# Expert results added on chip by one-hot products, the last fourteen experts in pairs, the overflow loop at the end

## The chip, the core and the metric

One core of a Trainium2 chip runs the whole program. TensorE (PE) multiplies and transposes into eight PSUM banks, VectorE (DVE) and ScalarE (ACT) move and change what lies there, GpSimd (POOL) issues the indirect transfers, and SyncE (SP) issues the weight loads. Each engine takes its instructions in a fixed order. The metric is the device time of one execution in microseconds (us), and less is better.

## The reference

512 tokens of 1024 numbers go through a mixer, a mixture of experts, and a second block of two feed-forwards with attention between them. The change touches the mixture of experts:

```python
def run_block(args):
    xb, e = args
    return (jax.nn.silu(xb @ w_gate[e]) * (xb @ w_up[e])) @ w_down[e]
...
y = y_pad[dest] * sorted_w[:, None].astype(h.dtype)
out = jnp.zeros((n_tok, d), h.dtype).at[sorted_tok].add(y)
```

Each token goes to 2 of 32 experts (1024 assignments); an expert has gate and up weights of 1024 x 512 and down weights of 512 x 1024. All is float32.

## The kernel before

The activations stand transposed in `self.x` ([128, 8, 512]: features on partitions, eight blocks k, tokens along the row). The router counts the tokens of each expert and ranks the experts by count. `SEQ` is the order in which the experts are worked: experts 0 and 1 (fixed, so that their weights can be loaded early), then four times two small experts and a big one, then eighteen small ones.

- **Big** (ranks 0 to 5): 128 slots, products as three float32r matmuls (`mm3`, L255 to L257) on weights that ACT and DVE split into a high and a low half (`wtile`, L201 and L202).
- **Small** (ranks 6 to 31): 64 slots, plain float32 on the raw weights. The array is used as two halves of 64 columns: gate and up (`small_up`, L960), or the two output halves (`small_down`, L987), lie side by side in one bank. The profile shows each of these matmuls as two instructions.

The loop `for n, p in enumerate(SEQ)` (in `moe`) does for each expert: transpose the activation (`small_tr` L972, copied by DVE L975), start the gather of the tokens of expert n+2 (POOL L1061), transpose the tokens of expert n+1 (`small_x` L944, copied by DVE L947), do its up products, then the down products of expert n. ACT scales the result out of PSUM (L991), and POOL scatters its rows to a DRAM array `yrow` (L877), which SP had cleared during the mixer (`clear`). The results of the last three experts stay on chip. At the end `yrow` is read back, its two halves are added (L869), transposed (L1023) and added to `x`; the last three results are added by a one-hot product (`add_block`, L1013 and L1014): a matrix `sel` of 0 and 1 (`one_hot`, L1039 to L1044) carries slots back to tokens. The last result is fed into `x` block by block inside the first feed-forward (`ffn`).

The weights of an expert are six transfers of 1 MB (`mload`, L236) that SP issues in the order `wkeys`, up to 13 ahead, into the 16 buffers of `p8`; one of the 16 holds the gathered tokens. `spill` is a loop over all experts for tokens past the slots. With the reference's inputs it runs no round: the largest counts of the ranks do not pass the slots. Its entry stands after expert n = 22.

Of the kernel before, what the change touches and what calls it, by code (L numbers as in the profile page):

```python
# [9 lines left out]
I32 = mybir.dt.int32  # L10
# [22 lines left out]
NFIXED, NBIG, CAP = 2, 6, 64  # L33
ROUNDS = (T + CAP) // 128 + 1
MOE_WINDOW = 13
MOE_MORE = {0: 8, 3: 9, 5: 10, 6: 11, 7: 12}
LAST = 3
# [4 lines left out]
def sequence():  # L42

    small = list(range(NBIG, NE))
    seq = list(range(NFIXED))
    for b in range(NFIXED, NBIG):
        seq += [small.pop(0), small.pop(0), b]
    return seq + small


SEQ = sequence()
RAW = 2
# [6 lines left out]
SPILL_AT = 22  # L59
# [55 lines left out]
class Net:  # L115
    def __init__(self, tc, ctx, A, out):
# [24 lines left out]
        self.yrow = self.dr.tile([2 * T, D], F32, name="yrow")  # L141
# [188 lines left out]
    def mixer(self):  # L330
# [53 lines left out]
        for c in range(ND):  # L384
            self.clear(c)
# [167 lines left out]
    def clear(self, j):  # L553

        if j == 0:
            self.zero = self.t4([128, D])
            self.nc.gpsimd.memset(self.zero, 0.0)
        self.tc.keep_in_program_order(self.nc.sync.dma_start(self.yrow[j * 128:j * 128 + 128, :], self.zero))

# [48 lines left out]
    def moe_stream(self):  # L608
# [5 lines left out]
        for n, p in enumerate(SEQ):  # L614
            gu = [("gu"[j], p, h) for h in range(2) for j in range(2)]
            d = [("d", SEQ[n - 1], h) for h in range(2)] if n else []
            self.wkeys += d + gu if n == NFIXED else gu + d
        self.wkeys += [("d", SEQ[-1], h) for h in range(2)]
        self.windex = {k: i for i, k in enumerate(self.wkeys)}
        views, last = [], None  # L620
        for p in SEQ + [None]:
            if p is not None and p < NBIG:
# [6 lines left out]
        self.mload(MOE_MORE[0])  # L629

# [33 lines left out]
    def moe(self):  # L664
# [9 lines left out]
        hrow, yrow, table, pay, payf = self.hrow, self.yrow, self.table, self.pay, self.payf  # L674
# [82 lines left out]
        def fixed2(e):  # L757

            p = self.ps()
            for i in range(NT):  # L760
                mm(p[:, 0:3], sels[e].bitcast(F32)[:, i, :], payf[:, i, e, 0:3], start=i == 0, stop=i == NT - 1)
            nc.vector.tensor_scalar(tabs[e][:, 1:2], p[:, 0:1], float(FAR), None, op0=add)
            nc.vector.tensor_copy(tabs[e].bitcast(F32)[:, 2:4], p[:, 1:3])
# [3 lines left out]
        rank, order, big = self.ranks(cn)  # L767
# [9 lines left out]
        pf = [payf[:, :, :, c] for c in range(3)]  # L777
        nc.vector.tensor_scalar(pf[0], o2[:, :, fx], float(T), None, op0=mul)
        nc.vector.tensor_tensor(pf[0], pf[0], self.payi.bitcast(F32)[:, :, 0:1].to_broadcast([128, NT, NFIXED]), op=add)
        nc.vector.tensor_tensor(pf[2], o2[:, :, fx], bc(d, NFIXED), op=mul)  # L780
        nc.vector.tensor_tensor(pf[1], o1[:, :, fx], bc(ds, NFIXED), op=mul)
        nc.vector.tensor_tensor(pf[1], pf[1], pf[2], op=add)
        nc.vector.tensor_copy(pf[2], rt.rearrange("p (i o) -> p i o", o=1).to_broadcast([128, NT, NFIXED]))
# [7 lines left out]
        nc.vector.scalar_tensor_tensor(rowr, rk3, CAP - 0.5, all4(big), op0=ALU.is_ge, op1=mul)  # L791
        nc.vector.tensor_tensor(rowr, rowr, all4(rank), op=add)
        nc.vector.scalar_tensor_tensor(row, rk3, float(NE), rowr, op0=mul, op1=add)
# [23 lines left out]
        nc.vector.tensor_scalar(ce, cn[:, 0:NE], CAP + 0.5, None, op0=ALU.is_gt)  # L817
        nc.vector.scalar_tensor_tensor(ce, big, 1.0 / NE, ce, op0=mul, op1=mul)
# [11 lines left out]
        tab2 = self.keep("tab2", [128, NE, 4], I32)  # L830
        for h in range(2):
            nc.gpsimd.dma_start(tab2[64 * h:64 * h + 64].rearrange("p e c -> p (e c)"), trow[0:64, :])
        nc.gpsimd.dma_start(self.ordd, order[0:1, :])
        for p in range(NFIXED, NE):
            tabs[p] = tabb[:, p, :] if p < NBIG else tab2[:, p, :]

        def gather(n):
            p = SEQ[n]
# [5 lines left out]
        def up(n):  # L844
            p, xt = SEQ[n], self.xts[n % 2]
            if p < NBIG:
                return self.expert_up(self.split_next, self.expert_x(xt), tabs[p])
            return self.small_up(p, self.small_x(xt), tabs[p])
        a = up(0)
        last, ys = [], []  # L850
        for n, p in enumerate(SEQ):
            tab = tabs[p]
# [5 lines left out]
            if n == NE - LAST:  # L858
                for i in range(NT):
                    ya = self.t8([128, 2, D])  # L860
                    nc.gpsimd.dma_start(ya, yrow.rearrange("(j i p) d -> i p j d", j=2, p=128)[i])
                    ys.append(ya)
            if n == NE - 2:
# [3 lines left out]
            if n == NE - 1:  # L867
                for ya in ys:
                    tc.keep_in_program_order(nc.vector.tensor_tensor(ya[:, 0], ya[:, 0], ya[:, 1], op=add))  # L869
                self.add_rows(ys)  # L870
                self.add_small(last)
            if p < NBIG:
                y, tb = self.expert_down(self.split_next, aT, tab), tab
            else:
                y, tb = self.small_down(p, aT, tab), tab[0:CAP]
            if n < NE - LAST:
                nc.gpsimd.indirect_dma_start(yrow, bass.IndirectOffsetOnAxis(ap=tb[:, 1:2], axis=0), y, None,  # L877
                                             bounds_check=2 * T - 1, oob_is_err=False)
            else:
                last.append(self.small_rows(y, tab))  # L880
            if n == SPILL_AT:
                self.spill(rounds, trow)
            self.presplit(self.wnext + SPLITS)
        self.last = last[LAST - 1:]

    def spill(self, rounds, trow):
# [3 lines left out]
        with tc.For_i(1, nr, 1) as b:  # L890
            with tc.For_i(0, NE, 1) as p:
                A, B, C = (self.t8([128, 2048], dt) for dt in (F32R, F32, F32))
                P, Q = self.t2(), self.t2()
                G, Y = self.t4([128, 1024], F32R), self.t4([128, 1024])
                U, V = ([self.wp.tile([128, 2, 512], F32R, name=nm, tag=nm) for nm in ("wh", "wl")] for _ in range(2))
                X, Z = self.ps(), self.ps()
                self.own = {"t8": [A, B, C, B, C, B, C, A], "t4": [G, Y], "t2": [P, Q, G[:, 0:512]],
# [11 lines left out]
                self.add_experts([self.expert_rows(self.expert_down(st.__next__, aT, tb), tb)])  # L909
                self.own = None  # L910

    def ranks(self, cn):
# [21 lines left out]
        rank, big = self.keep("rank", [128, NE]), self.keep("big", [128, NE])  # L934
        nc.vector.tensor_copy(rank, p[:, NE:2 * NE])
        nc.vector.tensor_scalar(big, rank, NBIG - 0.5, float((128 - CAP) * NE), op0=ALU.is_ge, op1=mul)
        return rank, self.order, big
# [12 lines left out]
    def small_up(self, e, xT, tab):  # L950
# [27 lines left out]
    def small_down(self, e, aT, tab):  # L978
        nc = self.nc
        tf = tab.bitcast(F32)  # L980
        p = self.ps()
        for h in range(2):
            w = self.raw_next(("d", e, h))
            for q in range(2):
                k = 2 * h + q
                for j in range(2):
                    nc.tensor.matmul(p[CAP * j:CAP * j + CAP, :], aT[:, k * CAP:k * CAP + CAP],  # L987
                                     w[:, q, j * 512:j * 512 + 512], start=k == 0, stop=k == 3)
        y = self.t4([128, D])
# [4 lines left out]
    def small_rows(self, y, tab):  # L994

        nc = self.nc
        sel = self.one_hot(tab)
        both = self.t8([128, 2, D], F32R)
        yT, hi = both[:, 0], both[:, 1]
        nc.scalar.copy(hi[0:CAP], y)  # L1000
        nc.vector.tensor_tensor(yT[CAP:128], y, hi[0:CAP].bitcast(F32), op=ALU.subtract)
        nc.scalar.copy(yT[0:CAP], y)
        return yT, sel
# [11 lines left out]

    def add_rows(self, ys):

        nc = self.nc
        for i, ya in enumerate(ys):
            for h in range(2):  # L1020
                p = self.ps()
                for k in range(4):
                    nc.tensor.transpose(p[:, k * 128:k * 128 + 128],  # L1023
                                        ya[:, 0, (4 * h + k) * 128:(4 * h + k) * 128 + 128], self.ident)
# [698 lines left out]
```

## Time and profile before

| | us |
|---|---|
| median of 3 runs (2073.02 to 2077.95) | 2075.43 |
| the profiled execution, its own time | 2075.37 |
| its span, first to last instruction | 2073.6 |
| PE busy | 1917.7 (92%) |
| DVE busy | 1145.2 (55%) |
| ACT busy | 736.0 (35%) |
| mixture of experts, about | 455 to 1010 |

Busy shares are averages over stages. In the stage of the experts the profile gives 410 GB/s of transfers, elsewhere mostly 20 to 110. The profiled execution is within 0.1 us of the median.

### The profile page before, as it was taken

How to read it: one execution, taken by the hardware profiler on the slowest of the kernel's cores; microseconds unless marked ns; L12 is line 12 of the kernel's file. 1: busy time of each engine (PE TensorE's matmuls, PEld its weight loads, DVE VectorE, ACT ScalarE, POOL GpSimd, SP SyncE). 2: the span in 40 equal slices, each digit the busy share in tenths (PEclk: the TensorE clock that was granted, in tenths of full speed). 3: DMA queues.
4: the chain of work that ended last, by engine and by line, in shares of the span. 5: the costliest groups of instructions: out<-in, count | busy, mean ns of one | idle time of the engine just before them, and what ended most of it. 6: DMA issues, size and time to landing. Idle time of an engine off the chain costs nothing.

```text
span 2073.6 us, 24135 instructions
## 1 busy us (share of the span) xinstructions
PE 1917.7 (92%) x9267; PEld 1429.9 (69%) x9267; DVE 1145.2 (55%) x1905; ACT 736.0 (35%) x1143; POOL 86.4 (4%) x106
## 2 busy tenths in 40 slices
PE   7999999979988998496799999999989999999997
PEld 5898888866444432132688888888777778888886
DVE  7999987456444311011864443248999855444323
ACT  5334335336333311011432322235448543232221
POOL 0000001002111111010000000000000000000000
PEclk9999999979999999698899999999999999999998
DMA  9121233539999999798222224230111112222311
GB/s 332 52 102 41 102 122 111 228 112 343 406 409 413 406 408 412 315 418 368 82 83 100 92 92 156 97 133 19 49 31 62 47 69 90 101 92 92 147 56 41
DMA packets 65463, 354.15 MB, mean 171 GB/s; under 512 B 10523, under 2 KB 11451, under 8 KB 32832
## 3 DMA queue, kind: packets, MB, share of 16 engines
q1 hardware_dynamic: 56304, 334.06, 41.6%
q0 software_dynamic: 7744, 14.71, 2.1%
q10 hardware_dynamic: 1296, 3.79, 0.5%
q8 instruction: 74, 1.21, 0.2%
q14 instruction: 45, 0.37, 0.1%
HBM read 345.41 MB, written 17.91 MB: 175 GB/s over the span
## 4 chain that ended last, share of the span: by engine, by line
PE 48%; DVE 3%; DMA 3%; ACT 2%; issue 1%; DVEq 0%; ACTq 0%; SPq 0%
PE ps L255 14%; PE ps L257 14%; PE ps L256 14%; DMA t<-in_w_up 2%; PE ps L960 2%; PE ps L1564 1%; DMA t<-in_w_down 1%; PE ps L987 1%; ACT t L1538 1%; PE ps L1551 1%; DVE wl L202 0%; DVE t L202 0%; ACT wh L201 0%; ACT t L201 0%; PE ps L1569 0%
## 5 line engine op out<-in xcount | busy, mean ns | idle before, releaser
L255 PE MATMUL ps<-t,wl 128*128 128x512 f32 x1728 | 685.3, 397 | 16.8 <-ACT t L206 16.4
L256 PE MATMUL ps<-t,wh 128*128 128x512 f32 x1728 | 681.4, 394 | 1.0 <-DVE t L207 1.0
L257 PE MATMUL ps<-t,wh 128*128 128x512 f32 x1728 | 681.6, 394 | 0.0
L201 ACT CAST wh<-t 128x1024 fp32r<-128x1024 f32 (+3 forms) x321 | 325.4, 1016 | 697.1 <-PE ps L257 511.8
L202 DVE TENSOR_TENSOR wl<-t,wh 128x1024 fp32r<-128x1024 f32 (+3 forms) x321 | 379.0, 1182 | 237.3 <-ACT wh L201 233.3
L255 PEld LDWEIGHTS ps<-t,wl 128*128 128x128 f32 x1728 | 325.8, 189 | 94.8 <-ACT t L206 16.8
L256 PEld LDWEIGHTS ps<-t,wh 128*128 128x128 f32 x1728 | 326.0, 189 | 76.1 <-DVE t L207 1.5
L257 PEld LDWEIGHTS ps<-t,wh 128*128 128x128 f32 x1728 | 325.6, 188 | 75.8
L960 PE MATMUL ps<-t,t 128*64 128x512 f32 x832 | 202.0, 617 | 35.3 <-DVE t L947 15.8
L960 PEld LDWEIGHTS ps<-t,t 128*64 128x64 f32 x832 | 64.3, 141 | 156.6 <-issue 106.0
L402 DVE SCALAR_TENSOR_TENSOR t<-t,vec,t 128x512 f32<-128x512 f32 x240 | 165.4, 743 | 0.4
L255 PE MATMUL ps<-wh,t 128*128 128x256 f32 (+2 forms) x440 | 144.6, 329 | 8.3 <-DVE t L202 8.3
L965 DVE SCALAR_TENSOR_TENSOR t<-ps,tab,t 64x512 f32<-64x512 f32 x26 | 19.6, 756 | 233.8 <-ACT t L963 233.8
L256 PE MATMUL ps<-wl,t 128*128 128x256 f32 (+2 forms) x440 | 142.8, 325 | 0.0
L257 PE MATMUL ps<-wh,t 128*128 128x256 f32 (+2 forms) x440 | 141.9, 322 | 0.0
L963 ACT ACTIVATE t<-ps,tab 64x512 f32<-64x512 f32 x26 | 17.7, 681 | 239.8 <-PE ps L960 239.8
L987 PE MATMUL ps<-t,t 128*64 128x512 f32 x416 | 100.1, 596 | 2.2 <-DMA t<-in_w_down 2.2
L255 PEld LDWEIGHTS ps<-wh,t 128*128 128x128 f32 x440 | 83.7, 190 | 21.2 <-DVE t L202 9.9
L1195 DVE TENSOR_TENSOR t<-ps,rbc 128x512 f32<-128x512 f32 x44 | 30.3, 689 | 115.2 <-PE ps L257 115.2
L257 PEld LDWEIGHTS ps<-wh,t 128*128 128x128 f32 x440 | 83.7, 190 | 7.0
L256 PEld LDWEIGHTS ps<-wl,t 128*128 128x128 f32 x440 | 83.8, 190 | 6.4 <-DVE wl L202 0.2
L201 ACT CAST t<-t 128x512 fp32r<-128x512 f32 (+2 forms) x102 | 62.7, 620 | 56.9 <-DVE t L1196 26.6
(323 smaller groups left out, 1557.5 us busy)
## 6 DMA issues: line engine op xcount, KB each, us to landing
t<-in_w_down SPq DMA_DIRECT2D x80, 1024.0 KB, 16.1
t<-in_w_gate SPq DMA_DIRECT2D x64, 1024.0 KB, 19.7
t<-in_w_up SPq DMA_DIRECT2D x64, 1024.0 KB, 17.8
t<-in_w_in SPq DMA_DIRECT2D x24, 1024.0 KB, 6.0
t<-in_w_gate SPq DMA_DIRECT2D x44, 512.0 KB, 3.5
t<-in_w_up SPq DMA_DIRECT2D x44, 512.0 KB, 3.5
t<-in_w_down SPq DMA_DIRECT2D x8, 768.0 KB, 4.5
t<-in_w_qi SPq DMA_DIRECT2D x4, 1040.0 KB, 4.7
```

What stands on the lines that cost most here:

```text
L201: nc.scalar.copy(hi, src)
L202: nc.vector.tensor_tensor(lo, src, hi.bitcast(F32), op=ALU.subtract)
L255: mm(acc, a[1], b[0], start=first, stop=False)
L256: mm(acc, a[0], b[1], start=False, stop=False)
L257: mm(acc, a[0], b[0], start=False, stop=last)
L402: nc.vector.scalar_tensor_tensor(y[c], src, w, y[c], op0=mul, op1=add)
L960: nc.tensor.matmul(p[CAP * j:CAP * j + CAP, :], xT[:, k * CAP:k * CAP + CAP], ws[j][:, q, :], start=k == 0, stop=k == ND - 1)
L987: nc.tensor.matmul(p[CAP * j:CAP * j + CAP, :], aT[:, k * CAP:k * CAP + CAP], w[:, q, j * 512:j * 512 + 512], start=k == 0, stop=k == 3)
L1195: nc.vector.tensor_tensor(a, accs[1], rbc, op=mul)
L1538: nc.scalar.activation(part(i), part(i), AF.Exp, bias=nm[:, i:i + 1], scale=scale, accum_out=su[:, i:i + 1])
L1551: nc.tensor.transpose(tb[b][:, o + (i - s) * 128:o + (i - s) * 128 + 128], P[:, self.PO[i] + s * 128:self.PO[i] + s * 128 + 128], self.ident)
L1564: self.nc.tensor.matmul(acc[64 * h:64 * h + 64, s * 128:512], V[h](s), PT[h][:, self.SO[s]:self.SO[s] + 512 - s * 128], start=s == 0, stop ...
```

## The change

1. **Results stay on chip.** `yrow`, its clearing, the scatter and the read back are gone. A small result is split into a high half (ACT) and a low half (DVE) that fill 128 partitions, a big one into two tiles. In the next iteration DVE makes its one-hot matrix, and the up products of the expert after next carry, after each block k, the add of block k: a 128x512 matmul (two for a big result) and a DVE add into `x`.
2. **Pairs.** Ranks 18 to 31 run as seven pairs, 32 slots for each expert, four array parts of 32 columns side by side. So there are 25 units in place of 32.
3. **The overflow loop** stands between the up and the down products of the last unit, after the last weights and two feed-forward weights were asked for.

```diff
+    small = [(p,) for p in range(NBIG, NSMALL)]
+    seq = [(p,) for p in range(NFIXED)]
     for b in range(NFIXED, NBIG):
-        seq += [small.pop(0), small.pop(0), b]
-    return seq + small
+        seq += [small.pop(0), small.pop(0), (b,)]
+    return seq + small + [(p, p + 1) for p in range(NSMALL, NE, 2)]
...
-            self.clear(c)
...
+            ys = []
+            if y is not None:
+                sel = self.one_hot(tabs[SEQ[n - 1][0]])
+                ys = [(t, sel) for t in y]
             aT = self.expert_tr(a) if p < NBIG else self.small_tr(a)
-            if n + AHEAD < NE:
+            if n + AHEAD < NU:
                 gather(n + AHEAD)
-            if n + 1 < NE:
-                a = up(n + 1)
...
+            if n + 1 < NU:
+                a = up(n + 1, ys)
+            else:
                 self.fst = self.ffn_stream(A["w1_gate"], A["w1_up"], A["w1_down"])
                 self.fst.load(FFN_FIRST)
-                self.fst.split(2)
...
+                self.add_small(ys)
+                self.fst.split(1)
+                for key in self.down_keys(unit):
+                    self.raw_next(key)
                 self.spill(rounds, trow)
+            y = self.expert_down(self.split_next, aT, tab) if p < NBIG else self.small_down(unit, aT, tab)
...
+        c = CAP // len(unit)
         for h in range(2):
-            ws = [self.raw_next((nm, e, h)) for nm in "gu"]
+            ws = [(CAP * j + c * i, c * i, self.raw_next(("gu"[j], e, h))) for i, e in enumerate(unit) for j in range(2)]
             for q in range(4):
                 k = 4 * h + q
-                for j in range(2):
-                    nc.tensor.matmul(p[CAP * j:CAP * j + CAP, :], xT[:, k * CAP:k * CAP + CAP], ws[j][:, q, :],
+                for o, i, w in ws:
+                    nc.tensor.matmul(p[o:o + c, :], xT[:, k * CAP + i:k * CAP + i + c], w[:, q, :],
                                      start=k == 0, stop=k == ND - 1)
+                also(k)
...
+        y = self.t4([128, D], F32R)
         for j in range(2):
-            nc.scalar.mul(y[0:CAP, j * 512:j * 512 + 512], p[CAP * j:CAP * j + CAP], tf[CAP * j:CAP * j + CAP, 2:3])
-        return y[0:CAP]
...
+            nc.scalar.mul(y[s, c], p[s], w2[s])
+            nc.vector.scalar_tensor_tensor(y[o, c], p[s], w2[s], y[s, c].bitcast(F32), op0=ALU.mult,
+                                           op1=ALU.subtract)
+        return [y]
```

**On DVE**, from one small expert to the next. Before, between the gating product (L965) and the copy of the next tokens (L947) there is one copy of the activation (L975):

```order
L965 SCALAR_TENSOR_TENSOR t_5682<-ps,tab_3628,t_5680 64x512
L975 COPY t_5708<-ps 128x256
L947 COPY t_5722<-ps 128x512
L965 SCALAR_TENSOR_TENSOR t_5760<-ps,tab_3628,t_5758 64x512
L975 COPY t_5786<-ps 128x256
L947 COPY t_5800<-ps 128x512
```

Now the low half of the result (L999) and the one-hot matrix (L1018 to L1023) stand ahead of both copies (the tokens' copy is L944 here), and the eight adds (L1012) behind them:

```order
L965 SCALAR_TENSOR_TENSOR t_5944<-ps,tab_3617,t_5942 64x512
L999 SCALAR_TENSOR_TENSOR t_5959<-ps,tab_3617,t_5959 64x512 x2
L1018 TENSOR_SCALAR tokf<-tab_3617 128x1
L1020 TENSOR_SCALAR toff<-cc,tokf 128x4
L1023 TENSOR_SCALAR t_5968<-cc,toff 128x128 x4
L975 COPY t_5978<-ps 128x256
L944 COPY t_5992<-ps 128x512
L1012 TENSOR_TENSOR x<-x,ps 128x512 x8
L965 SCALAR_TENSOR_TENSOR t_6063<-ps,tab_3617,t_6061 64x512
```

The copy that the next up products read has moved behind eight instructions that belong to the result before.

**On PE**, the up products of one small expert. Before, the two halves follow one another, all with 64 columns:

```order
L972 MATMUL ps<-cc,t_5760 128x64 x4
L944 MATMUL ps<-cc,t_3001 128x64 x8
L987 MATMUL ps<-t_5613,t_5708 64x512 x4
L960 MATMUL ps<-t_5656,t_5800 64x512
L960 MATMUL ps<-t_5658,t_5800 64x512
L960 MATMUL ps<-t_5656,t_5800 64x512
L960 MATMUL ps<-t_5658,t_5800 64x512
```

Now a 128-column add (L1011) stands after each two (L959 are the up, L992 the down products):

```order
L992 MATMUL ps<-t_5826,t_5978 64x512 x4
L972 MATMUL ps<-cc,t_6063 128x64 x4
L941 MATMUL ps<-cc,t_2990 128x64 x8
L959 MATMUL ps<-t_5886,t_6111 64x512
L959 MATMUL ps<-t_5888,t_6111 64x512
L1011 MATMUL ps<-t_6087,t_6078 128x512
L959 MATMUL ps<-t_5886,t_6111 64x512
L959 MATMUL ps<-t_5888,t_6111 64x512
L1011 MATMUL ps<-t_6087,t_6078 128x512
```

So PE goes from 64-column parts to the whole array and back eight times in an expert.

**On PE at the end of the experts.** Before, the read-back rows are transposed (L1023) and two results added (L1013) ahead of the last down products. Now the add of the unit before (L1011) and the entry of the overflow loop (L882, L883) stand there:

```order
L1011 MATMUL ps<-t_7224,t_7215 128x512 x8
L882 TENSOR_LOAD rounds
L883 COMPARE_AND_BRANCH
L883 UNCONDITIONAL_BRANCH x2
...
L992 MATMUL ps<-t_7130,t_7234 32x512 x2
L992 MATMUL ps<-t_7132,t_7234 32x512 x2
```

The 32 transposes are gone, and the loop's entry came from n = 22 to here.

## Rows read from the trace of the kernel before

**Rows 1.** Windows: busy of PE, PEld, DVE, ACT, POOL, then PE clock, transfer share, GB/s.

```profile
566.00:613.00 47.00, 41.88 (x204) 22.98 (x204) 19.94 (x21) 19.23 (x24) 6.50 (x8) 0.99 1.01 410
760.00:838.00 78.00, 64.47 (x288) 21.75 (x286) 8.24 (x13) 10.80 (x17) 8.37 (x9) 1.00 1.02 412
850.00:870.00 20.00, 3.14 (x16) 1.88 (x18) 1.12 (x2) 0.00 (x0) 0.96 (x1) 0.50 0.42 163
```

**Rows 2.** Waits of PE from 519 to 711 us: total, times, longest.

```profile
PE ps L960 <- DVE t L947: 12.6, 8, 3.8
PE ps L255 <- DVE t L202: 5.6, 4, 1.4
```

**Rows 3.** Timeline, one small expert to the next: start, length, engine, what, idle before.

```profile
927.19 3.63 PE L987 MATMUL ps<-t,t 128*64 128x512 f32 x16
...
928.14 0.76 DVE L965 SCALAR_TENSOR_TENSOR t<-ps,tab,t 64x512 f32<-64x512 f32 x1 [7.95 <-ACT t L963]
...
930.86 1.38 ACT L991 ACTIVATE t<-ps,tab 64x512 f32<-64x512 f32 x2 [2.75 <-PE ps L987]
...
931.24 0.42 DVE L975 COPY t<-ps 128x256 f32<-128x256 f32 x1 [2.34 <-PE ps L972]
...
931.75 0.69 DVE L947 COPY t<-ps 128x512 f32<-128x512 f32 x1
...
932.54 7.09 PE L960 MATMUL ps<-t,t 128*64 128x512 f32 x32 [0.83 <-ACT t L991]
...
939.43 1.92 PE L987 MATMUL ps<-t,t 128*64 128x512 f32 x8
```

**Rows 4.** Timeline of PE, up products of small experts, 519 to 749 us.

```profile
519.30 7.09 PE L960 MATMUL ps<-t,t 128*64 128x512 f32 x32 [1.16 <-DVE t L947]
...
566.05 7.09 PE L960 MATMUL ps<-t,t 128*64 128x512 f32 x32 [1.16 <-DVE t L947]
...
613.91 9.31 PE L960 MATMUL ps<-t,t 128*64 128x512 f32 x32 [3.79 <-DVE t L947]
...
646.46 7.09 PE L960 MATMUL ps<-t,t 128*64 128x512 f32 x32 [0.78 <-DVE t L947]
...
663.58 10.07 PE L960 MATMUL ps<-t,t 128*64 128x512 f32 x32 [3.37 <-DVE t L947]
...
748.15 7.09 PE L960 MATMUL ps<-t,t 128*64 128x512 f32 x32 [0.83 <-ACT t L991]
```

**Rows 5.** Timeline of DVE: first and last instructions of one one-hot matrix.

```profile
952.54 0.15 DVE L1039 TENSOR_SCALAR tokf<-tab 128x1 f32<-128x1 int32 x1
...
953.00 0.88 DVE L1044 TENSOR_SCALAR t<-cc,toff 128x128 fp32r<-128x128 f32 x4
```

**Rows 6.** Timeline of PE where 64-column products give way to 128-column ones.

```profile
510.44 1.03 PE L960 MATMUL ps<-t,t 128*64 128x512 f32 x4
...
511.39 0.50 PE L255 MATMUL ps<-wh,t 128*128 128x512 f32 x1
...
511.73 0.39 PE L256 MATMUL ps<-wl,t 128*128 128x512 f32 x1
```

**Rows 7.** Timeline of PE at the overflow loop.

```profile
866.08 0.69 PE L972 MATMUL ps<-cc,t 64*128 64x64 f32 x4 [28.96 <-SPq L890]
```

**Rows 8.** Timeline of PE, end of the experts and start of the feed-forward.

```profile
968.98 1.94 PE L987 MATMUL ps<-t,t 128*64 128x512 f32 x8 [1.49 <-DMA t<-in_w_down]
...
995.15 3.97 PE L1013 MATMUL ps<-t,t 128*128 128x512 f32 x16
...
999.05 3.65 PE L987 MATMUL ps<-t,t 128*64 128x512 f32 x16
...
1006.61 0.47 PE L1013 MATMUL ps<-t,t 128*128 128x512 f32 x1 [3.90 <-DVE t L1001]
...
1015.44 0.39 PE L255 MATMUL ps<-t,wl 128*128 128x512 f32 x1
```

**Rows 9.** Timeline of POOL, first gather after the tables.

```profile
484.98 0.99 POOL L1061 DMA_INDIRECT t<-hrow,tab  x1 [4.51 <-PE ps L1071]
```

More of the change, by code (lines that the diff above doesn't have):

```diff
@@ L42, in sequence @@
 def sequence():
[L44 to L45 removed]
+    small = [(p,) for p in range(NBIG, NSMALL)]
+    seq = [(p,) for p in range(NFIXED)]
     for b in range(NFIXED, NBIG):
[L47 to L48 removed]
+        seq += [small.pop(0), small.pop(0), (b,)]
+    return seq + small + [(p, p + 1) for p in range(NSMALL, NE, 2)]
 SEQ = sequence()
+NU = len(SEQ)
 RAW = 2
@@ L629, in moe_stream, with down_keys @@
         self.mload(MOE_MORE[0])
+    def down_keys(self, unit):
+        return [("d", p, h) for h in range(2) for p in unit]
     def mload(self, n):
@@ L673, in moe @@
         rt = self.rstd([self.hsq], D, "rtok")
-        hrow, yrow, table, pay, payf = self.hrow, self.yrow, self.table, self.pay, self.payf
+        hrow, table, pay, payf = self.hrow, self.table, self.pay, self.payf
         for i in range(NT):
@@ L766, in moe @@
             self.gather(self.xts[e], tabs[e])
-        rank, order, big = self.ranks(cn)
+        rank, order, less = self.ranks(cn)
         gs = small("gs", 1)
@@ L776, in moe @@
         nc.vector.tensor_tensor(d, ds, d, op=mul)
[L777 to L783, printed above, removed]
+        pf = [payf[:, :, :, c] for c in range(2)]
+        nc.vector.tensor_tensor(pf[1], o2[:, :, fx], bc(d, NFIXED), op=mul)
+        nc.vector.tensor_tensor(pf[0], o1[:, :, fx], bc(ds, NFIXED), op=mul)
+        nc.vector.tensor_tensor(pf[0], pf[0], pf[1], op=add)
+        nc.vector.tensor_copy(pf[1], rt.rearrange("p (i o) -> p i o", o=1).to_broadcast([128, NT, NFIXED]))
         for e in range(NFIXED):
@@ L790, in all4 @@
             return t.rearrange("p (o e) -> p o e", o=1).to_broadcast([128, NT, NE])
-        nc.vector.scalar_tensor_tensor(rowr, rk3, CAP - 0.5, all4(big), op0=ALU.is_ge, op1=mul)
-        nc.vector.tensor_tensor(rowr, rowr, all4(rank), op=add)
-        nc.vector.scalar_tensor_tensor(row, rk3, float(NE), rowr, op0=mul, op1=add)
+        nc.vector.tensor_tensor(rowr, rk3, all4(less), op=add)
+        nc.vector.scalar_tensor_tensor(rowr, rowr, 127.5, all4(less), op0=ALU.is_ge, op1=mul)
+        nc.vector.tensor_tensor(rowr, rowr, rk3, op=add)
+        nc.vector.scalar_tensor_tensor(row, rowr, float(NE), all4(rank), op0=mul, op1=add)
         payfl = pay.bitcast(F32)
@@ L816, in moe @@
         ce = self.keep("ce", [128, NE])
-        nc.vector.tensor_scalar(ce, cn[:, 0:NE], CAP + 0.5, None, op0=ALU.is_gt)
-        nc.vector.scalar_tensor_tensor(ce, big, 1.0 / NE, ce, op0=mul, op1=mul)
+        nc.vector.tensor_tensor(ce, cn[:, 0:NE], less, op=add)
+        nc.vector.scalar_tensor_tensor(ce, ce, 128.5, less, op0=ALU.is_gt, op1=mul)
         nc.vector.tensor_tensor(ce, cn[:, 0:NE], ce, op=add)
@@ L842, in gather, with up, also @@
                 self.gather(self.xts[n % 2][0:CAP], tabs[p][0:CAP])
[L844 to L848, printed above, removed]
-        a = up(0)
-        last, ys = [], []
-        for n, p in enumerate(SEQ):
-            tab = tabs[p]
+        def up(n, ys=()):
+            unit, xt = SEQ[n], self.xts[n % 2]
+            tab = tabs[unit[0]]
+            def also(k):
+                if ys:
+                    self.add_block(ys, k)
+            if unit[0] < NBIG:
+                return self.expert_up(self.split_next, self.expert_x(xt), tab, also)
+            return self.small_up(unit, self.small_x(xt), tab, also)
@@ L867, in moe @@
[L867 to L880, printed above, removed]
@@ L933, in ranks @@
         nc.vector.tensor_copy(self.order, p[:, 0:NE])
-        rank, big = self.keep("rank", [128, NE]), self.keep("big", [128, NE])
+        rank, less, t = (self.keep(nm, [128, NE]) for nm in ("rank", "less", "lesst"))
         nc.vector.tensor_copy(rank, p[:, NE:2 * NE])
-        nc.vector.tensor_scalar(big, rank, NBIG - 0.5, float((128 - CAP) * NE), op0=ALU.is_ge, op1=mul)
-        return rank, self.order, big
+        nc.vector.tensor_scalar(less, rank, NBIG - 0.5, 64.0, op0=ALU.is_ge, op1=mul)
+        nc.vector.tensor_scalar(t, rank, NSMALL - 0.5, 32.0, op0=ALU.is_ge, op1=mul)
+        nc.vector.tensor_tensor(less, less, t, op=add)
+        return rank, self.order, less
     def small_x(self, xt):
@@ L948, in small_x, with small_up @@
         return xT
-    def small_up(self, e, xT, tab):
+    def small_up(self, unit, xT, tab, also):
         nc = self.nc
@@ L1046, in one_hot @@
         return sel
-    def add_experts(self, ys):
-        nc = self.nc
-        n = 2 * len(ys)
-        for k in range(ND):
-            p = self.ps()
-            for j in range(n):
-                yT, sel = ys[j // 2]
-                nc.tensor.matmul(p, yT[:, 1 - j % 2, k * 128:k * 128 + 128], sel, start=j == 0, stop=j == n - 1)
-            nc.vector.tensor_tensor(self.x[:, k, :], self.x[:, k, :], p, op=ALU.add)
     def gather(self, xt, tab):
```

119 lines of the change are left out of this document (50 added, 69 removed).

## The prediction

> **What bounds the kernel now.** I read the windows by stage first. In the stage of the experts the transfers are busy all the time (share 1.01 to 1.02 at 410 to 412 GB/s), and PE is busy for 41.88 of 47 us and 64.47 of 78 us [rows 1]. Both are near full, so I asked what PE waits for. In the first part, with the big experts, the list of waits names no transfer, only DVE: 12.6 us for the copy of the tokens, 5.6 us for the split tokens of a big expert [rows 2]. So there the chain of PE and DVE sets the pace, with the transfers just keeping up.
>
> How long that chain is shows in the timeline. From one small expert's down products to the next's, with the weights there, it is 939.43 - 927.19 = 12.24 us [rows 3]: down 3.63, then 1.72 us until the next up starts, in which DVE copies the activation and the tokens, then 6.9 us of up. The weights of an expert are 6 x 1.05 MB, at 412 GB/s 15.3 us (2.55 us for each). So PE and DVE have 3 us to spare for each small expert. A group of two small and one big takes 566.05 - 519.30 = 46.75 us in its clean form [rows 4], against 3 x 15.3 = 45.9 us of weights: nothing to spare. This is the place to cost the change: what it adds to the chain of a unit, and what the weights' buffers can hide.
>
> **Parts that cost nothing, and their cover.** The clearing of `yrow` lies in the mixer, where the engines don't read it; without it nothing waits less. POOL issues four more table loads before the first gather; I take 0.99 us for each, that of a gather, and the 4.51 us that POOL idles there [rows 9] cover them; without cover they would cost 4 us once. SP reads all ranks' expert numbers early; it does so up to 13 transfers ahead. The fixed experts' tables lose an instruction or two.
>
> **What each up product gains, on PE.** A result's add is eight 128x512 matmuls: sixteen took 3.97 us [rows 8], so 0.25 each, 2.0 us for a small result and 4.0 for a big one.
>
> PE also changes between 64-column parts and the whole array, eight times there and back. One way: the last pairs start 0.43 us apart, from 510.44 and 510.87 the next slot is 511.30; the 128-column product starts at 511.39 and its follower 0.34 later in place of 0.23 [rows 6], so 0.20. The other way: sixteen adds from 995.15 would leave the next slot at 998.97, and the 64-column product starts at 999.05 [rows 8]; with the slower second pair I take 0.13. Together 0.33, times 8 = 2.6 us for a small expert; for a big one nothing, its products have 128 columns. Below lies 0, if this is paid only where other waits hide it; above, double, if the early loading of weights is lost too. [...]
>
> **What the hand-over gains, on DVE.** The order shows that the tokens' copy now waits behind the low half of the result and its one-hot matrix, and these wait for the down products. Worked from the end of down at 930.82 with rows 3: ACT's first half 0.04 + 0.69 (1.38 for two), two DVE halves of 0.76 (the length of L965, which has that form), the one-hot matrix 953.88 - 952.54 = 1.34 [rows 5], copies 0.42 + 0.69, 0.1 to PE: 935.6, where up started at 932.54. That is 3.1 us more, with PE idle. Next to a big expert a split of weights may stand in between too; I leave it out. Into a big expert the order puts the tokens' split ahead of the one-hot matrix; there I add nothing.
>
> **What the longer idle costs in clock.** After short hand-overs (0.78 and 1.16 us idle) up takes 7.09 us. [...]
>
> **Sum until the first pair.** A small up with a small result added: 2.0 + 2.6 + 3.1 + 2.6 = 10.3 us; with a big result 12.3; a big up 2.0. From unit 2 to the first pair (unit 18) there are 6, 6 and 4 of these, and the hand-over into the pair: 61.8 + 73.8 + 8 + 3.1 = 147 us. The two long waits of before with their slow ups go away (about 5 us saved net). So the first pair's up starts 142 us after 748.15 [rows 4], at 890.
>
> A small expert then takes 22.5 us and a group 71 us, far above the 15.3 and 45.9 of their weights. The transfers run ahead until all 15 free buffers hold weights, then idle.
>
> **The pairs.** At 890, of the 86 transfers still to be used (7 x 12 and the 2 down weights of unit 17) 15 have landed; 71 x 2.55 = 181 us bring the last at 1071. PE keeps up if four 32-column parts run together as two do now: 22.5 us for a pair against 12 x 2.55 = 30.6. If they ran two by two, up and down would take 6.9 + 3.6 more: 33.0, and I add 7 x 2.4 = 17 us; I take the first. The removed scatter (at most 4.2 MB, 10 us) and the stall of the transfers at the overflow loop (20 us x 0.58 = 11.6 us lost [rows 1]) would have helped only where transfers are the bound: the 181 us have neither in them.
>
> **The end.** Before, from the last weights at 968.98 it is 46.5 us to a full stream of the feed-forward at 1015.44 [rows 8]: waiting for the read-back, transposes, adds. After: the two feed-forward weights 2.5 us (1 MB), the loop's entry 3 us (an estimate; transfers had drained a little before PE came back at 866.08 [rows 7]), down products 6 us at the low clock, result and one-hot 3.7, and the 8.8 us from 1006.61 to 1015.44 as now: 24 us. That is 22 us saved. The stream starts at 1071 + 24 = 1095, 79.5 us later than before; from there on nothing changes. On the profiled 2075.4, which is the median, this gives **2155 us**.
>
> In short, the end and the loop give back some 62 us in all (1015.44 - 748.15 - 181 - 24), and what the units before the pairs lose beyond that is the loss: lag - 62.
>
> **The rivals.**
>
> *The modes change freely and the clock holds* (chance 0.12). For it: one up after 1.16 us idle kept its clock, and TensorE can load weights ahead. Against it: rows 4 and 6. Then 12 x (2.6 + 2.6) = 62 us fall away: 2093.
>
> *The transfers stay the bound* (0.14), the other side. This needs the new hand-over to lie under other work, so that each of the 16 units before the pairs gains less than 62 / 16 = 3.9 us; from there it decides. For it: the transfers are full now, and a small expert has 3 us to spare. Against it: adds of 2 to 4 us and a hand-over of 3.1 are in the order of the instructions, already 5 and more. The last weight would land at 968.98 - 11.6 - 10 = 947, the stream start at 971: 44 us faster, 2031.
>
> *Pairs run two by two* (0.10): 2172. [...] No row here has four parts.
>
> *The change also runs the overflow loop* (0.02): an expert of rank 18 or later with over 32 tokens would bring a round over 32 experts, 32 x 15.3 = 490 us: about 2640. The reference's own inputs give these ranks at most 20 tokens.
>
> **How the numbers follow.** My forecast, a slower kernel at 2155, has 0.59; 0.03 go to no change, between the rivals (lag near 62). Its own range comes from the clock (0 to 3.0), the modes (0 to double) and the buffers (three more or fewer, 8 us): 2110 to 2200 when not all err one way. The full range reaches down past the free-mode rival to 2085 and up to 2200; below it lie the transfer-bound case and no change, above it the loop, 0.19 in all. Faster by over 0.2% (about what a measurement of this kernel can tell) 0.14, within it 0.03, slower 0.83.
>
> **What the profile after would show.** Right: from 530 to 890 us a transfer share near 0.65, PE waiting for the copy of the tokens some 3 to 4 us in each unit, small experts 20 to 23 us apart, a clock below 1 in these windows; in the pairs a share of 1.0 and PE waiting for weights; no wait at the old place of the loop, and about 24 us from the last weight to the full stream. Wrong: small experts 15 to 16 us apart and a transfer share of 1.0 from 530 on (then the hand-over is hidden), or ups of about 9 us with adds in them (then modes and clock are free), or pairs over 31 us apart with the weights there.

## The result, and the profile after

The changed kernel takes 2153.52 us (median of 4 runs, 2150.93 to 2158.33), the kernel before 2076.65 us beside it: ratio 1.0376, 95% interval 1.0352 to 1.0399. It is 3.8% slower, and 1.5 us from the 2155 predicted. The profiled execution has a span of 2151.2 us.

The windows by stage, of the same stretches as [rows 1] and then of the two parts of the stage (columns as there):

```profile
566.00:613.00 47.00, 38.23 (x147) 15.90 (x146) 29.26 (x47) 11.29 (x14) 1.93 (x2) 0.85 0.74 282
760.00:838.00 78.00, 65.62 (x256) 29.43 (x254) 45.48 (x79) 17.73 (x22) 3.72 (x4) 0.87 0.71 270
850.00:870.00 20.00, 15.46 (x48) 4.12 (x50) 9.70 (x19) 1.36 (x2) 0.93 (x1) 0.83 0.68 256
530.00:890.00 360.00, 304.64 (x1218) 131.03 (x1218) 210.82 (x351) 83.61 (x103) 15.10 (x16) 0.89 0.72 276
890.00:1059.00 169.00, 119.10 (x722) 34.69 (x722) 60.01 (x117) 12.95 (x19) 3.72 (x4) 0.89 1.01 419
```

Where the transfers were full before, their share is now 0.72 until the pairs begin; from then on it is 1.01. DVE is busy for 29.26 of 47 us where it was for 19.94. The clock is below 1 in all of them. In the third stretch the stall of the overflow loop is gone.

PE's waits from 519 to 711 us, as in [rows 2] (total, times, longest):

```profile
PE ps L959 <- DVE t L944: 22.3, 5, 4.7
PE ps L255 <- DVE t L202: 2.9, 3, 1.0
```

Five waits for the tokens' copy take 22.3 us, 4.5 each, where eight took 12.6. One hand-over between two single experts shows why, in the timeline, as in [rows 3]. In the changed kernel L992 are the down products, L998 and L999 the result's halves on ACT and DVE, L1018 to L1023 the one-hot matrix, L975 and L944 the copies of activation and tokens, L959 the up, L1011 and L1012 the adds on PE and DVE:

```profile
825.77 0.60 PE L992 MATMUL ps<-t,t 128*64 128x512 f32 x2
...
826.42 0.69 ACT L998 ACTIVATE t<-ps,tab 64x512 fp32r<-64x512 f32 x1 [3.54 <-PE ps L992]
...
827.14 0.74 DVE L999 SCALAR_TENSOR_TENSOR t<-ps,tab,t 64x512 fp32r<-64x512 f32 x1 [2.84 <-ACT t L998]
...
827.91 0.68 ACT L998 ACTIVATE t<-ps,tab 64x512 fp32r<-64x512 f32 x1 [0.81 <-DVE t L999]
828.63 0.76 DVE L999 SCALAR_TENSOR_TENSOR t<-ps,tab,t 64x512 fp32r<-64x512 f32 x1 [0.75 <-ACT t L998]
...
829.86 0.87 DVE L1023 TENSOR_SCALAR t<-cc,toff 128x128 fp32r<-128x128 f32 x4
830.76 0.42 DVE L975 COPY t<-ps 128x256 f32<-128x256 f32 x1
831.10 0.68 DVE L944 COPY t<-ps 128x512 f32<-128x512 f32 x1
...
831.84 1.98 PE L959 MATMUL ps<-t,t 128*64 128x512 f32 x4 [4.58 <-DVE t L944]
...
834.47 1.98 PE L959 MATMUL ps<-t,t 128*64 128x512 f32 x4
...
836.81 1.08 PE L959 MATMUL ps<-t,t 128*64 128x512 f32 x4
...
838.25 1.08 PE L959 MATMUL ps<-t,t 128*64 128x512 f32 x4
...
845.42 1.94 PE L992 MATMUL ps<-t,t 128*64 128x512 f32 x8
```

Down ends at 826.37, the next up starts at 831.84: 5.47 us, where it was 1.72. ACT's second half (827.91) waits for DVE's first, and the tokens' copy stands last. The up then has two steps of some 2.5 us (834.47 - 831.84 = 2.63, 836.81 - 834.47 = 2.34; granted clock 0.50 and 0.60) and six of 1.44 (838.25 - 836.81; clock 1.00), 0.58 above the 0.86 of a step without an add (6.89 / 8 in [rows 3]).

The end, as in [rows 8]:

```profile
1058.84 1.91 PE L992 MATMUL ps<-t,t 128*32 128x512 f32 x12 [1.42 <-DMA t<-in_w_down]
...
1065.31 3.54 PE L1011 MATMUL ps<-t,t 128*128 128x512 f32 x8 [4.56 <-DVE t L1023]
...
1066.11 4.87 DVE L1012 TENSOR_TENSOR x<-x,ps 128x512 f32<-128x512 f32 x8 [0.49 <-PE ps L1011]
...
1072.79 6.55 PE L992 MATMUL ps<-t,t 128*32 128x512 f32 x32 [3.95 <-DVEq L883]
...
1083.87 0.77 PE L1011 MATMUL ps<-t,t 128*128 128x512 f32 x1 [4.53 <-DVE t L1023]
...
1092.68 0.40 PE L256 MATMUL ps<-t,wh 128*128 128x512 f32 x1
```

The full stream of the feed-forward starts at 1092.7 where it started at 1015.44: 77.2 us later. That is the whole difference, 2151.2 - 2073.6 = 77.6 us of span.

### The profile page after: what moved, and what is told of

Read it like the earlier page. It is cut to its first block, busy times and chain, and to the rows that moved or that the text cites. A ratio compares the mean times of both kernels' runs of the same rounds, so it can differ in the third digit from the quotient of the medians.

```text
span 2151.2 us, 24425 instructions
## 1 busy us (share of the span) xinstructions
PE 1967.4 (91%) x9375; PEld 1420.6 (66%) x9375; DVE 1300.3 (60%) x2234; ACT 716.3 (33%) x1116; POOL 48.7 (2%) x69
## 5 line engine op out<-in xcount | busy, mean ns | idle before, releaser
L202 DVE TENSOR_TENSOR wl<-t,wh 128x1024 fp32r<-128x1024 f32 (+3 forms) x321 | 378.1, 1182 | 203.7 <-ACT wh L201 201.0
L257 PEld LDWEIGHTS ps<-t,wh 128*128 128x128 f32 x1728 | 325.4, 188 | 76.1
L959 PE MATMUL ps<-t,t 128*32 128x512 f32 (+1 forms) x832 | 201.8, 696 | 93.5 <-DVE t L944 87.6
L1012 DVE TENSOR_TENSOR x<-x,ps 128x512 f32<-128x512 f32 x200 | 133.0, 685 | 163.4 <-PE ps L1011 163.4
L1011 PEld LDWEIGHTS ps<-t,t 128*128 128x128 f32 x248 | 48.2, 215 | 145.5 <-issue 129.7
L959 PEld LDWEIGHTS ps<-t,t 128*32 128x32 f32 (+1 forms) x832 | 35.6, 133 | 159.8 <-DVE t L944 93.3
L963 ACT ACTIVATE t<-ps,tab 64x512 f32<-64x512 f32 x19 | 12.9, 681 | 338.1 <-PE ps L959 338.1
L1011 PE MATMUL ps<-t,t 128*128 128x512 f32 x248 | 108.5, 505 | 9.1 <-DVE t L1023 9.1
L992 PE MATMUL ps<-t,t 128*32 128x512 f32 (+1 forms) x416 | 80.0, 629 | 8.6 <-DMA t<-in_w_down 4.7
```

Of the source, the lines that this page charges most:

```text
L202: nc.vector.tensor_tensor(lo, src, hi.bitcast(F32), op=ALU.subtract)
L257: mm(acc, a[0], b[0], start=False, stop=last)
L959: nc.tensor.matmul(p[o:o + c, :], xT[:, k * CAP + i:k * CAP + i + c], w[:, q, :], start=k == 0, stop=k == ND - 1)
L992: nc.tensor.matmul(p[o:o + c, :], aT[:, k * CAP + i:k * CAP + i + c], w[:, q, j * 512:j * 512 + 512], start=k == 0, stop=k == 3)
L1011: self.nc.tensor.matmul(p, yT[:, k * 128:k * 128 + 128], sel, start=j == 0, stop=j == n - 1)
L1012: self.nc.vector.tensor_tensor(self.x[:, k, :], self.x[:, k, :], p, op=ALU.add)
```

## The experiments

**The theory.** Each unit before the pairs costs PE and DVE more than its weights take to come: adds, eight changes of mode (from 64-column parts to the whole array and back), a hand-over with DVE in it, and the clock that falls in the wait. What is lost until the first pair comes back only in part. **Rivals:** modes and clock are free; the transfers, the pairs or the loop did it. Each run is timed against the kernel before on the same chip (medians 2076.24, 2075.99 and 2077.24 in the three series of four kernels, in the order below).

| run | us (median) | ratio to before, 95% interval |
|---|---|---|
| the change | 2153.52 | 1.0376 [1.0352, 1.0399] |
| noadd | 2047.75 | 0.9862 [0.9845, 0.9878] |
| parts16 | 2118.15 | 1.0211 [1.0193, 1.0229] |
| late | 2127.02 | 1.0244 [1.0227, 1.0261] |
| warm | 2166.28 | 1.0430 [1.0412, 1.0447] |
| warm5 | 2129.36 | 1.0260 [1.0243, 1.0277] |
| mixed | 2155.19 | 1.0381 [1.0363, 1.0398] |
| first_late | 2084.93 | 1.0042 [1.0030, 1.0055] |
| first_late_mixed | 2048.36 | 0.9865 [0.9849, 0.9882] |
| mixed3 | 2117.44 | 1.0199 [1.0182, 1.0216] |
| best3 | 2073.74 | 0.9987 [0.9977, 0.9997] |
| best3_mixed | 2051.34 | 0.9887 [0.9870, 0.9903] |
| loop_in | 2157.11 | 1.0392 [1.0374, 1.0409] |

**noadd: the price of adding at all.**

```diff
+                if n + 1 == NU:
                     sel = self.one_hot(tabs[SEQ[n - 1][0]])
                     ys = [(t, sel) for t in y]
```

> Leaves out the adds to x of all units but the next to last and the last, with their one-hot matrices; the two halves of each result are still made. Theory (chain of the units before the pairs): each small up loses 2.0 us of adds, 2.6 us of mode changes and 1.34 us of one-hot matrix, 5.9 of 10.3 us; the lag at the first pair falls from 130 to about 50 us, a single expert takes 16 to 17 us in place of 22.7, and the time is about 2063 (down to 2031 if the shorter idle also keeps the clock; then the transfers are full from 530 on). Rival (the pairs, the moved loop or the halves on DVE made it slower): within 15 us of 2153.

2048, some 15 us under the 2063 expected and faster than before. A window of it:

```profile
530.00:830.00 300.00, 253.62 (x1254) 119.62 (x1251) 114.20 (x135) 87.14 (x109) 16.02 (x17) 0.94 0.97 386
```

And PE's waits from 500 to 860 us (L960 is the up here; the lines of the experiments are shifted by a few):

```profile
PE ps L960 <- DVE t L945: 21.7, 11, 2.5
PE ps L960 <- DMA t<-in_w_up: 11.4, 10, 2.3
```

The share is back at 0.97, and PE waits for weights as well as for DVE. So the pairs, the moved loop and the halves are not what made the kernel slower; the adds and what comes with them are. With weights there, a single expert takes 12.9 us.

**parts16 and late: the modes, taken away in two ways.** In the first the adds run in the parts of the ups:

```diff
-            self.nc.tensor.matmul(p, yT[:, k * 128:k * 128 + 128], sel, ...)
+            for o in range(0, 128, c):
+                self.nc.tensor.matmul(p[o:o + c, :], yT[:, k * 128 + o:k * 128 + o + c], sel, ...)
```

> The adds inside small ups run as products of the width of the ups themselves (two 64-column or four 32-column parts), so PE changes no mode there; results and one-hot matrices are bfloat16 for it (the halves keep about 16 bits of the result). Same number of adds, same order. Theory: a step of a small up goes from 1.43 to 1.10 us, 2.6 us less for each of the 12 small ups before the pairs, 31 us in all: about 2122. Rival (the modes change freely and the 0.57 us of an add in a step is the add itself): step 1.43, time 2153.

In the second they stand behind the up, after `a` is made:

```diff
                     nc.tensor.matmul(p[o:o + c, :], ...)
-                also(k)
...
         nc.vector.scalar_tensor_tensor(a[0:CAP], ...)
+        for k in range(ND):
+            also(k)
```

> The eight adds stand in one row behind a small up in place of one behind each step. Theory: one change of mode there and back in place of eight, 7 x 0.33 = 2.3 us less for each of the 12 small ups before the pairs; the hand-over stays: about 2126. Rival (modes are free): 2153; it may be slower if the down products now wait for the eight adds' banks on DVE (8 x 0.67 us).

Both came out as the theory has it: 35 and 27 us less. PE in parts16, three steps with an add each:

```profile
809.42 1.02 PE L960 MATMUL ps<-t,t 128*64 128x512 f32 x4
810.28 0.38 PE L1013 MATMUL ps<-t,t 128*64 128x512 bf16 x2
810.49 1.03 PE L960 MATMUL ps<-t,t 128*64 128x512 f32 x4
811.35 0.38 PE L1013 MATMUL ps<-t,t 128*64 128x512 bf16 x2
811.57 1.02 PE L960 MATMUL ps<-t,t 128*64 128x512 f32 x4
```

A step is 1.07 us in place of 1.44 with the add still in it. Parts16 also changes the type of the adds, so by itself it might show a type; late keeps the type and the number and gains nearly as much. But with the changes of width late also saves changes of type. Parts16 still goes from f32 to bf16 and back at each step without the price; whether float32r has a share in it, or the loading of a 128-column weight, no run separates. The up of late and its adds:

```profile
811.53 9.68 PE L959 MATMUL ps<-t,t 128*64 128x512 f32 x32 [4.64 <-DVE t L944]
821.14 2.11 PE L1012 MATMUL ps<-t,t 128*128 128x512 f32 x8
```

Eight adds take 2.07 us (823.21, the next down, less 821.14), 0.26 each. The up without them takes 9.68 us after 4.64 us of waiting, and 7.09 in [rows 4] after short waits. I put these 2.6 us down to the clock, which in the changed kernel stood at 0.50 and 0.60 in the two steps after such a wait (above).

**warm and warm5: the clock, with the wait left in.** Extra products on constants fill the wait, ten in warm and five in warm5:

```diff
+        if len(unit) == 1:
+            p = self.ps()
+            for i in range(10):
+                nc.tensor.matmul(p[0:CAP, 0:456], self.cc[:, 0:CAP], self.cc[:, 0:456], start=True, stop=True)
```

> Ten extra 64-column products on constants (3.8 us at full clock) stand between the tokens' transposes and a single small expert's up, where PE waits 4.6 us for DVE. Theory: they run in the wait, the clock stays 1, and an up loses its slow first steps: 2.1 to 2.6 us less for each of the 12 small ups before the pairs, 25 to 31 us: about 2125, granted clock near 1 from 530 to 860. Rival (the slow first steps come from something other than the idle, or clock costs nothing): 2153 or, as the extra products get in the way, more.

2166, slower than the changed kernel. Ten filled 7.5 us, more than the wait: each is two passes on PE, and I had counted one. (In the row below five products stand as ten.) The slow steps were gone (from 799.23 to 807.84 us the steps of an up take 1.43 to 1.45 us, and the granted clock is 1.00 from 550 to 850 us), but the overhang cost more.

> As the run with ten extra products, with five: one of them took 0.76 us there and not 0.38, so that ten filled 7.5 us, 2.9 us more than the wait of 4.6. Five take 3.8 us and end within the wait. Theory: the clock stays 1 and each of the 12 small ups before the pairs loses its slow first steps, 1.5 to 2.4 us, 18 to 29 us in all: 2124 to 2135. Rival (the clock level costs nothing on the path, since the first steps are slow for another reason): 2153.

2129, in the range. PE in warm5:

```profile
807.13 4.04 PE L955 MATMUL ps<-cc 128*64 128x456 f32 x10
811.78 1.08 PE L963 MATMUL ps<-t,t 128*64 128x512 f32 x4 [0.61 <-DVE t L944]
812.78 0.49 PE L1015 MATMUL ps<-t,t 128*128 128x512 f32 x1
813.21 1.08 PE L963 MATMUL ps<-t,t 128*64 128x512 f32 x4
```

The first step takes 1.43 us (813.21 - 811.78) like the others, the mean clock from 530 to 860 us is 0.99 where the changed kernel has 0.89, and 24 us are gained, though the up still starts 5.5 us after the down (811.78, and 802.66 + 3.65). The clock is a cost of its own. The two windows, the changed kernel first:

```profile
530.00:860.00 330.00, 279.27 (x1100) 124.40 (x1102) 197.43 (x328) 81.57 (x100) 14.17 (x15) 0.89 0.73 278
530.00:860.00 330.00, 316.86 (x1298) 138.88 (x1296) 207.20 (x346) 82.81 (x102) 14.20 (x15) 0.99 0.78 298
```

**first_late: the hand-over.** On top of late, the result's halves and the one-hot matrix (a function `evict`, called later) come after the tokens' copy:

```diff
-                sel = self.one_hot(tabs[SEQ[n - 1][0]])
-                ys = [(t, sel) for t in y]
...
+            xT = self.expert_x(xt) if unit[0] < NBIG else self.small_x(xt)
+            adds = self.evict(*ys) if ys else ()
```

> Two parts of the hand-over undone: the tokens' transposes and copy stand ahead of the result's two halves and the one-hot matrix on DVE, and the eight adds stand in one row behind a small up. Theory: modes -2.3 us, hand-over -3.2 to -3.7 us, clock -1.5 to -2.4 us for each of the 12 small ups: 84 to 100 us less lag, 30 to 46 us in place of 130, less than the 62 us that the end and the loop give back: about 2045 to 2060, faster than before, wait for the tokens' copy about 1 us. Rival (DVE is now the bound of a unit with its 0.69 us adds, or the adds behind the up wait for the halves): 2100 or more.

42 us less than late, but 2085 where 2045 to 2060 were expected. PE's waits for DVE, in the changed kernel from 500 to 860 us, and in first_late from 500 to 1080 (L963 is the up and L948 the copy there, L202 the split tokens of a big expert):

```profile
PE ps L959 <- DVE t L944: 51.6, 12, 4.8
...
PE ps L963 <- DVE t L948: 13.2, 12, 1.7
PE ps L255 <- DVE t L202: 13.8, 4, 3.8
```

Waits for the copy fell from 51.6 us in 12 to 13.2 in 12. With the hand-over much of the clock's loss goes too (granted clock 0.93 to 1.00 in windows of 50 us from 500 to 800 us, 0.86 to 0.93 in the changed kernel); no run takes the hand-over away alone. The edit had put two other places wrong: DVE's order now had the one-hot matrix ahead of a big expert's split tokens (PE waits 3.8 us there, 1.0 before the edit), and at the end a split of feed-forward weights, which waits for the loop on ACT, ahead of the last one-hot matrix (PE waits 12.4 us).

**best3** puts these right: the split of tokens is held ahead of the one-hot matrix, and the splits of weights are called behind the up.

> The run with copies first and grouped adds, with three places put right: into a big expert the split of its tokens stands ahead of the one-hot matrix, the splits of weights stand behind the up, and at the last unit the one-hot matrix stands ahead of the feed-forward's split, which waits for the loop's entry. Theory (those places cost 5 us in each of four groups and 8 us at the end): 2085 - 28 = 2050 to 2060. Rival (the chain is as short as it gets, PE's own work bounds the first part): 2080 to 2085.

11 us less, where 25 to 35 were expected: 2073.74, 0.1% under before. The 8 us at the end came in full. The 5 us per group did not: a group takes 58.1 us where first_late's take 58.9 on the mean, and PE still waits 2.5 us at each big expert. The trace shows one reason: the two halves of the result still stand on DVE ahead of the split of the tokens (at one big expert they end at 598.73, the split starts at 598.76, PE at 599.50). Whether that is all that holds a group was not tried.

**The lag is carried to the end one to one.** POOL's gather for unit 20 starts as the first pair's tokens are transposed. Its time in the runs that keep the order of units, and the time of the run, both less the changed kernel's (loop_in is left out, as its loop stands behind this gather):

| run | gather of unit 20 | less 873.41 | time less 2153.5 |
|---|---|---|---|
| parts16 | 839.57 | -33.8 | -35.4 |
| late | 848.67 | -24.7 | -26.5 |
| warm | 888.77 | +15.4 | +12.8 |
| warm5 | 848.67 | -24.7 | -24.2 |
| first_late | 800.00 | -73.4 | -68.6 |
| best3 | 797.27 | -76.1 | -79.8 |
| noadd | 768.70 | -104.7 | -105.8 |

What a unit loses before the pairs is the kernel's loss, to a few us.

**mixed and mixed3: only the order of units.**

```diff
-        seq += [small.pop(0), small.pop(0), (b,)]
-    return seq + small + [(p, p + 1) for p in range(NSMALL, NE, 2)]
+        seq += [small.pop(0), pairs.pop(0), small.pop(0), (b,)]
+    while small:
+        seq += [u.pop(0) for u in (small, pairs) if u]
+    return seq + pairs
```

> The same units in another order: the seven pairs stand between the small experts instead of behind them. The same work, the same bytes. Theory (first part bound by the chain of PE and DVE with the transfers idle a quarter of the time, the pairs bound by the transfers): each pair then hides 30.6 us of transfers behind others' chains and costs its own 22.5 us: the last 7 pairs' 181 us become 7 x 22.5 = 157 us, 24 us less: about 2130, transfer share even at 0.85 to 0.9. Rival (one bound all through, be it transfers or the chain): the order doesn't matter, 2153.

Nothing gained: 2155, as the rival said. But the share from 530 to 890 us rose from 0.72 to 0.86, so one bound all through it was not. DVE in a hand-over of mixed, with the up that waits for it:

```profile
746.67 0.76 DVE L1002 SCALAR_TENSOR_TENSOR t<-ps,tab,t 64x512 fp32r<-64x512 f32 x1 [0.75 <-ACT t L1001]
...
747.74 1.23 DVE L205 TENSOR_TENSOR wl<-t,wh 128x1024 fp32r<-128x1024 f32 x1 [0.31 <-ACT wh L204]
...
749.35 1.23 DVE L205 TENSOR_TENSOR wl<-t,wh 128x1024 fp32r<-128x1024 f32 x1 [0.39 <-ACT wh L204]
...
750.55 1.22 DVE L205 TENSOR_TENSOR wl<-t,wh 128x1024 fp32r<-128x1024 f32 x1
...
751.94 0.87 DVE L1026 TENSOR_SCALAR t<-cc,toff 128x128 fp32r<-128x128 f32 x4
...
753.19 0.68 DVE L947 COPY t<-ps 128x512 f32<-128x512 f32 x1
...
753.92 1.98 PE L962 MATMUL ps<-t,t 128*64 128x512 f32 x4 [8.63 <-DVE t L947]
```

With other units around it, three splits of the next big expert's weights (L205) had come between the result's halves and the tokens' copy: the wait is 8.6 us, not 4.6, and a group of four takes 95.6 us. The scheduler had changed two things where I had changed one. mixed3 keeps the order of units and calls the splits behind the up:

> The order of units of the run with mixed pairs, with DVE's order in the hand-overs put back to what it is in the changed kernel: the splits of the next big expert's weights stand inside the second small up again and not ahead of the tokens' copy, and the split of a big expert's tokens stands ahead of the one-hot matrix. Theory (the order of units is worth 24 us, and in the run before it was lost again on DVE, 4 us in the hand-over with three splits ahead and 3 us in the one into a big expert, with their clock, four times): a group of small, pair, small, big takes 68.5 + 22.2 = 91 us in place of 95.6, and the time is 2125 to 2140. Rival (the order of units is worth nothing): 2153.

2117, below the range, 36 us less than the changed kernel. A group takes 88.8 us where 91 were expected. DVE's order around a big expert is not quite that of the changed kernel either, so the 36 us are not the order's alone; that the order is worth some 24 of them is borne out, not shown by itself.

**first_late_mixed and best3_mixed: both together.**

> Both edits of the run before and the pairs between the small experts. Theory: the chain of every unit then is within its weights' time taken over a few units, so the transfers are full from the first unit on, and the time is the floor: last weights at about 947, full stream 24 us later, 2031 to 2040. Rival (a wait of the chain remains that the order can't hide, or 15 buffers do not reach over a big expert): 2050 or more.

2048, 1.35% faster than before. The floor I gave was too low: the transfers are at the bound,

```profile
550.00:940.00 390.00, 334.38 (x1760) 167.90 (x1758) 250.65 (x436) 95.26 (x120) 16.98 (x18) 0.91 1.01 412
```

and the last weight of the experts lands at 954 us, 7 behind the 947 of the prediction's transfer rival. The full stream starts at 986.5, 32 us after it and not 24, since the last units' chains are still to run: PE's last adds start only at 960.7, after 5.6 us of waiting for a one-hot matrix.

> As the run before, with the pairs between the small experts. Theory: with that order the transfers were already full (share 1.01 from 550 to 930 us) and end at 949, so a shorter chain gives nothing before 949; only the end gains, 0 to 8 us: 2040 to 2048. Rival (the chain still bounds): 2020 to 2035.

2051, no better, 3 us above the range: where the transfers were full, a shorter chain was worth nothing. Neither run is told apart from the other by its interval.

**loop_in: the overflow loop back inside the stage**, at `n == NU - 5`.

> The changed kernel with the overflow loop back inside the stage, behind the down products of the third pair, where the transfers are full. Theory (the loop drains the transfers as before, 20 us at a share of 0.42, and the transfers bound this part): 11.6 us lost there, about 4 us less wait at the end: about 2161. Rival (the stall is made up by the buffers or was the end's cost anyway): 2145 to 2153.

3.6 us slower than the changed kernel, with intervals that overlap. The transfers drained less than in [rows 1]:

```profile
980.00:1000.00 20.00, 0.00 (x0) 0.00 (x0) 0.00 (x0) 0.00 (x0) 0.00 (x0) 0.50 0.89 370
1000.00:1020.00 20.00, 17.73 (x112) 5.23 (x116) 8.54 (x17) 0.68 (x1) 0.93 (x1) 0.79 0.79 312
```

20 x (0.11 + 0.21) = 6.4 us are lost in these two, not 11.6. The last weight is issued 8.3 us later than in the changed kernel (1057.30, 1048.98) and the profiled span is 4.6 us longer, so some 4 come back at the end, as expected. Where the loop stands is worth a few us here: during PE's wait of 27 us the buffers fill, and the next two pairs then start 22.6 us apart (1003.81, 1026.43), less than the 30.6 that the weights of one take to come.

## Why the prediction was right, point by point

**The bound moves to the chain: right.** Share 0.72 to 890 us (0.65 predicted), waits of 4 to 4.8 us for the copy, single experts 22.7 us apart (22.5), pairs at share 1.01. noadd takes the cause away and the loss with it. One sign was wrong: in the pairs (860 to 1060 us) PE waits more for DVE's copy (35.9 us, 7 times) than for weights (10.7 us, 9 times); that the transfers bound there shows in their share. What I took to cost nothing before the first gather cost nothing: it starts at 485.20, before at 484.98.

**Adds, 2.0 us a unit: right**, 2.07 in late.

**Modes, 2.6 us a unit: right.** An add within a step costs 0.57 to 0.58 us, 0.26 of it the product: 0.32 for the change there and back, times eight 2.6. In parts16, where no mode changes, a step is 0.37 shorter, 0.05 of it because its add takes 0.21 (1.07 - 0.86). Parts16 and late show that price on the path; what takes the time in a change, no run shows.

**Hand-over, 3.1 us: mis-sized, 3.75** between single experts (5.47 less 1.72). I let ACT do both halves in a row; its second half waits for DVE's first. In the groups the wait is 4.0 to 4.8 us where it was 0.8 to 1.2, so 3.2 to 3.6 more.

**Clock, 2.6 us: a little too much.** The term was my estimate from [rows 4]: the mean of the two ups after waits of over 3 us, 9.31 and 10.07, less 7.09; the 3.0 of the range comes from the larger one. In the changed kernel the up from 831.84 to 845.42 takes 13.58 us and eight full steps 11.5: 2.1. warm5 gains 24 us over the 12 ups, 2.0 each, with the mean clock at 0.99 and not 0.89.

**The lag, 142 us: 130.** The first pair's up starts at 877.77. A group took 68.4 us (gathers at 643.14 and 711.52), not 71: my base of 46.75 for a clean group was 1.5 too long (551.13 to 596.36 is 45.2 in the same trace), and the clock's term too large. The four groups of before from 519.30 to 711.42 took 192.1 us, 11 more than four of 45.2, and I had taken off only 5 for the waits that go away.

**The transfers until the last weights: the 181 us began later than I said.** After 877.77 no buffer came free at once: SP's next issue is at 886.02, after four of the eight steps of the first pair's up, the first three of them slow:

```profile
878.00:884.00 6.00, 6.00 (x26) 0.98 (x18) 1.38 (x2) 0.00 (x0) 0.00 (x0) 0.50 0.43 139
884.00:890.00 6.00, 6.00 (x44) 1.37 (x36) 2.75 (x4) 0.00 (x0) 0.00 (x0) 0.99 0.48 176
890.00:896.00 6.00, 6.00 (x36) 1.96 (x33) 2.13 (x3) 0.94 (x2) 0.00 (x0) 1.00 1.01 426
```

They are full from 890 on, the time at which I had the pair start. From there 71 weights land, as counted, the last at 1068.7 (predicted 1071). The lag's 12 us and this delay, which I had left out, cancelled: that the total came within 1.5 us is luck to that extent.

**The end, 24 us: right** (1092.68 less 1068.7), and mostly in its parts. 4.1 from the last weight to the down products (5.5), 6.55 for down (6; granted clock 0.55 there), 4.5 to the first add (3.7), 8.8 to the full stream as before; PE leaves the loop's entry 1.8 us after DVE's eight adds end (1066.11 + 4.87); that DVE's adds stand ahead of the loop I had not seen. The 46.5 us of before I read wrongly: at 968.98 the last expert's two down weights were still to come (the transfers stay at 1.00 to 974 us), some 5 us more, so the end was shortened by less than the 22 us that I gave, and the 947 of the transfer rival was as much too early. The forecast uses neither.

**Pairs: four parts run together, right.** A pair's step with an add takes 1.42 us, a single expert's 1.44. Before the runs nothing showed it: no row of before has four parts, and I chose between two values.

**The rivals.** Free modes and clock: refuted by parts16, late and warm5 (35, 27 and 24 us less). Transfers as the bound: noadd (share 0.97) and the two runs with both edits (1.01) come near it; as its condition said, a unit may then gain only a few us.

## What to carry to other kernels

Work that is small for its engine can still be dear by where it stands: eight 0.26 us adds cost ten us a unit here, through a mode change each (0.32 us), through DVE work put ahead of a copy that TensorE waits for (3.75 us), and through the clock lost in that wait (2.0 to 2.1 us). Put such adds in a row behind the products, and the copy that the next products need first in line (first_late, 69 us less than the change). Here one part of the stage was bound by a chain (transfer share 0.72) and the next by transfers (1.01); in such a stage mix the units (mixed3 gained 36 us, some of it by DVE's order), and then look again at the order that the scheduler made of it.

## What the runs showed that I had not expected

Filling the waits of TensorE before the twelve single small ups with five useless products each made the kernel 24 us faster than leaving them idle (2129 against 2153). After 4.6 us of waiting the granted clock stood at 0.50 from 878 to 884 us in the first pair's up (above); after a filled wait the first step ran like the rest (1.43 us in warm5). And ACT and DVE did not overlap on the two halves of one result: each waited 0.75 to 0.81 us for the other (827.14 to 828.63 above), though they read different rows. The waits are on semaphores of the program; whether the chip needs that order no run shows.
